# A two-layer hybrid encoder: attention of branch A beside later products, other places for transposing round trips, splits in halves

## The chip, the cores and the metric

The kernel runs on one core of one Trainium2 chip. The core has a matrix engine (TensorE, PE), a vector engine (VectorE, DVE), an activation engine (ScalarE, ACT), a general engine (GpSimd, POOL) and an engine that issues DMAs (SyncE, SP). Each works through its own instructions in a fixed order and waits on semaphores for the others. The metric is the device time of one execution in microseconds.

## The reference

Two layers of a mixer over 256 tokens of width 2048, in float32. In each layer the input is normalised, and one product with `w_in` (2048 x 16192) feeds three attention branches and their gates:

```python
h = _rmsnorm(x, g_pre)
u = h @ w_in
qa = (_rmsnorm(a_cq, a_g_cq) @ a_w_uq)      # A: latent attention, 8 heads
kva = (_rmsnorm(a_ckv, a_g_ckv) @ a_w_ukv)
o_a = _mla_attention(qn, qr, kn, kr, kva[..., A_NOPE:])
o_b = _rmsnorm(_diff_attention(bq, bk, bv, lam), b_g_sub) * (1.0 - lam_init)
o_c = _chunk_band_attention(cq, ck, cv, c_rel_bias)
branches = (o_a * silu(a_z), o_b * silu(b_z), o_c * silu(c_z))
y = sum(gates[:, :, n] * (branches[n] @ w_branch[n]) for n in range(3))
x = x + y @ w_out
```

In A the queries and keys come from two low-rank latents (cq, ckv) by second products (uq, ukv); queries and keys are normalised per head and part of them is rotated. B subtracts a second softmax map per head. C adds a relative bias.

## The kernel before

All products go through `matunit` (L150). It takes weights as a stream in the order that `stream_plan` (L43) writes down: blocks of 256 rows by 512 columns, one block per **step**. For a step SP issues one DMA of 512 KB into one of four buffers, ACT casts it to the matrix engine's fp32r type (high part, L166), DVE subtracts to get the low part (L167; three buffers each), and PE runs 12 matmuls: for each of two 128-row halves and two token tiles high x high, high x low, low x high (L176 to L178). A unit of 2048 rows is 8 steps; a pair of PSUM banks holds its two token tiles, and there are two pairs.

A layer's units come in this order: cq and ckv (A's latents), az0 and az1 (A's gate, two halves of four heads), then the second products uq0, ur, uk0, uv0 (half 0) and uq1, uk1, uv1 (half 1); B's k, q, v and z of half 0 and of half 1 (b0k ... b1z); four times a gate of A with its branch product br0; C's eight units; the gates and branch products of B and of C; four units of the output product.

Behind a unit of queries or keys stands `qk_natural` (L295): copies and squares on ACT, sums and scaling on DVE, the power on POOL. Then the result is needed with features on the partitions. There are two ways: `to_transposed` (L211) on PE, and `bounce` (L230), a round trip over DRAM: DVE transposes 32x32 blocks, one DMA writes 512 KB, four DMAs of 128 KB read it back in another order, and `from_bounced` (L277) casts and splits it into high and low part on ACT and DVE. `bounce` gets three numbers, the steps after its call at which the write, the read and the use are handed out: `later` (L140) notes them, and `run_due` (L144) runs what is due in `matunit`, between a step's cast and its matmuls (L169). The write and the read stand in SP's order behind that step's weight load, the use in ACT's order behind that step's cast (`tc.issue_after`).

Attention is `simple_half` (L428; A and C) and `diff_half` (L447; B): per head scores on PE, maximum on DVE, Exp on ACT, scaling, transposes of the map and products with v on PE, and a product with the gate. `silu_gate` (L342) makes that gate with Silu on ACT; `gate_branch` (L699) uses Sigmoid. `b_split` (L621) splits a finished branch for its branch product.

The code is traced from top to bottom, and a planner then fixes each engine's order before the run: earlier instructions have priority, and one that its model of times holds ready may go ahead of one that it holds not. What the order came to be can be read from the trace.

Of the kernel before, what the change touches and what calls it, by code (L numbers as in the profile page):

```python
# [8 lines left out]
F32 = mybir.dt.float32  # L9
# [9 lines left out]
NT = SEQ // P  # L19
# [23 lines left out]
def stream_plan():  # L43

    order = []
    for l in range(DEPTH):
        def win(name, lo, n):
            order.append(("w_in", l, lo, DM, n))
        win("cq", 0, 512)
        win("ckv", 512, 320)  # L50
        win("az", 832, 512)
        win("az", 832 + 512, 512)
        order.append(("uq", l, 0, 512, 512))
        order.append(("uq", l, 1024, 512, 512))
        order.append(("ukv", l, 0, 256, 512))
        order.append(("ukv", l, 1024, 256, 512))
        order.append(("uq", l, 512, 512, 512))
        order.append(("ukv", l, 512, 256, 512))
        order.append(("ukv", l, 1536, 256, 512))
        qb = 1856  # L60
        for hf in range(2):
            for s in (1, 0, 2, 3):
                win("b", qb + s * BW + hf * 512, 512)
        gb = 1856 + 8 * BW
        for j in range(4):
            win("g", gb + j * 512, 512)
            order.append(("br0", l, j * 512, BW, 512))
        qc = 1856 + 4 * BW
        for hf in range(2):
            for s in (1, 0, 3, 2):  # L70
                win("c", qc + s * BW + hf * 512, 512)
        for n in (1, 2):
            for j in range(4):
                win("g", gb + n * DM + j * 512, 512)
                order.append((f"br{n}", l, j * 512, BW, 512))
        for j in range(4):
            order.append(("out", l, j * 512, DM, 512))
    return order
# [3 lines left out]
def trunk_kernel(ctx: ExitStack, tc: tile.TileContext, x, xT, w, cols, rows, tab, bias, ident_d, out):  # L82
# [57 lines left out]
    def later(n, fn):  # L140

        due.append((state["n"] + n, fn))
# [87 lines left out]
    def bounce(src, name, at, then=None, dst=None):  # L230
# [23 lines left out]

        def use():
            with tc.issue_after(state["cast"].ins):
                then(flat)
            away.remove(name)

        later(at[0], write)  # L260
        later(at[1], read)
        if then is not None:
            later(at[2], use)
        return flat

    def bounced(z, b=None):

        v = z.rearrange("p (q b c) -> p q b c", b=HH, c=32)
        return v if b is None else v[:, :, b, :]

# [5 lines left out]

    def from_bounced(z, dh, dl, gain, per_block=False, put=None):  # L277

        if per_block:
            for b in range(HH):  # L280
                split(as_bounced(dh[:, b, :]), as_bounced(dl[:, b, :]), bounced(z, b), gain(b))
            return
        if gain is not None:
            nc.scalar.activation(z, z, AF.Copy, scale=gain)
        if put is not None:
            put(bounced(z), as_bounced)
        else:
            split(as_bounced(dh), as_bounced(dl), bounced(z))

# [46 lines left out]
    def vsplit(ps, rcol, name):  # L336
# [3 lines left out]
        return v  # L340

    def silu_gate(ps, rcol, name):  # L342
        z = zp.tile([P, NT, 512], F32, tag="z", name=name)
        for t in range(NT):
            nc.scalar.activation(z[:, t, :], ps[t], AF.Silu, scale=rcol[:, t:t + 1])
        return z
# [137 lines left out]
    for l in range(DEPTH):  # L484
# [85 lines left out]
        for t in range(NT):  # L570
# [6 lines left out]
        cqh, cql = abig[:, 0], abig[:, 1]  # L577
        bounce(ncq, f"cqT{l}", (9, 11, 14),
               lambda z: from_bounced(z, cqh, cql, lambda b: gcol(G_CQ + b), per_block=True))

# [40 lines left out]
        def b_split(z, hf, name, gain=None):  # L621
            bh[hf] = zp.tile([P, HH, SEQ], F32R, tag=f"bh{hf}", name=f"{name}h", bufs=1)
            bl[hf] = zp.tile([P, HH, SEQ], F32R, tag=f"bl{hf}", name=f"{name}l", bufs=1)
            assert not [x for x in away if x.startswith(name)]
            from_bounced(z, bh[hf], bl[hf], gain)

        za = [None, None]
        qr = [None, None]
        for hf in range(2):
            n = f"l{l}a{hf}"  # L630
            za[hf] = bounce(silu_gate(in_unit(f"az{hf}"), rcol, f"{n}z"), f"{n}zT", (7, 9))
        for hf in range(2):
            n = f"l{l}a{hf}"
            assert f"cqT{l}" not in away
# [19 lines left out]

            def parts(hl):
                qs = qr[hf][:, (hl % 2) * 2 + hl // 2, :]
                return [(qh[:, hl, :], kt2[:, :, hl, :], True), (qs, krt, True), (ql[:, hl, :], kt2[:, :, hl, :], False)]

            za[hf] = simple_half(za[hf], parts, v, lambda hl: mask_add, n)
        for hf in range(2):  # L660
            b_split(za[hf], hf, f"l{l}a{hf}")


        zb = [None, None]
        for hf in range(2):
            n = f"l{l}b{hf}"
            op = {}
            for i, nm in ((1, "k"), (0, "q")):
# [8 lines left out]
                else:  # L677
                    d = att_tile(f"{n}{nm}")
                    d = [d[:, 0], d[:, 1]]
                    put = lambda pt, v, d=d: split_stacked(v(d[0]), v(d[1]), pt)  # L680
                bounce(nat, f"{n}{nm}T", (11, 13, 15),
                       lambda z, i=i, put=put: from_bounced(z, None, None, cg[:, 1:2] if i == 0 else cg[:, 4:5], put=put))
                op[nm] = d
# [7 lines left out]
            diff_half(zb[hf], bparts, v, nlam, n)  # L691
            zb[hf] = bounce(zb[hf], f"{n}bT", (20, 22))

# [5 lines left out]
        def gate_branch(n):  # L699
            for j in range(4):  # L700
# [3 lines left out]
                g = wk.tile([P, NT, 512], F32, tag="g", name=f"{nm}g")  # L704
                for t in range(NT):
                    nc.scalar.activation(g[:, t, :], pg[t], AF.Sigmoid, scale=rcol[:, t:t + 1])
                pb = matunit(lambda kt: (bh[kt // 4][:, kt % 4, :], bl[kt // 4][:, kt % 4, :]), BW, 512, f"{nm}b")
# [6 lines left out]
                if n == 2:  # L714
                    yt = att_tile(f"{nm}y")
                    yh[j], yl[j] = yt[:, 0], yt[:, 1]
                    if j < 3:
                        yz = zp.tile([P, NT, 512], F32, tag="z", name=f"{nm}yz")
                        bounce(yacc[:, :, js], f"{nm}yT", (9, 11, 13),
                               lambda z, yt=yt: from_bounced(z, yt[:, 0], yt[:, 1], None), yz)  # L720
                    else:
                        to_transposed(lambda t: yacc[:, t, js], 4, yh[j], yl[j], None, f"{nm}yT")
# [7 lines left out]
        for hf in range(2):  # L730
# [8 lines left out]
            for i, nm in ((1, "k"), (0, "q")):  # L739
                nat = qk_natural(in_unit(f"c{hf}{nm}"), 128, rcol, f"{n}{nm}")  # L740
                th = op[nm] = att_tile(f"{n}{nm}")
                bounce(nat, f"{n}{nm}T", (8, 10, 12), lambda z, th=th, i=i: from_bounced(
                    z, th[:, 0], th[:, 1], cg[:, 2:3] if i == 0 else gcol(G_CKH)))
            zc[hf] = bounce(silu_gate(in_unit(f"c{hf}z"), rcol, f"{n}z"), f"{n}zT", (6, 8))
# [26 lines left out]
        for j in range(4):  # L771
# [11 lines left out]
            if more:  # L783
# [5 lines left out]
                if j < 3:  # L789
                    bounce(xres[:, :, js], f"x{l + 1}T{j}", (7, 9, 11),  # L790
                           lambda z, j=j, gx=gx: from_bounced(z, xg_next[0][j], xg_next[1][j], gx, per_block=True),
                           nat_pair(f"x{l + 1}n{j}"))
# [81 lines left out]
```

## Time and profile before

| | us |
|---|---|
| median of 3 runs (lowest to highest) | 2046.84 (2045.09 to 2046.86) |
| the profiled execution, its own time | 2047.27 |
| its span on the core | 2045.5 |
| PE busy | 1996.6 (98%) |
| DVE busy | 1262.2 (62%) |
| ACT busy | 1138.1 (56%) |
| POOL busy | 207.7 (10%) |

The span is what the trace covers; times of instructions are counted from its start. Busy is the share of the span in which an engine has an instruction in work; a matmul's end is modelled, so a busy PE may still run at its lower clock. The granted clock, 0.989 in the mean, is a share of full speed.

### The profile page before, as it was taken

What the parts mean: (1) busy time and instruction counts of PE and PEld (TensorE: products, weight loads), DVE (VectorE), ACT (ScalarE), POOL (GpSimd) and SP (SyncE); (2) the same over time, 40 slices, a digit from 0 to 9 for tenths busy, and PEclk for the clock granted to TensorE, in tenths of its full rate; (3) what the DMA queues carried; (4) which work ended last, traced back from release to release, by engine and by line L of the source; (5) the groups of instructions that cost most, each with busy time, mean ns of one, the idle gap of its engine ahead of it and who ended that gap; (6) DMA issues with size and microseconds to landing.
All of it is one profiled execution on the core that took longest, in us unless ns stands there. A gap on an engine that the chain in (4) does not pass through costs nothing.

```text
span 2045.5 us, 25426 instructions
## 1 busy us (share of the span) xinstructions
PE 1996.6 (98%) x9136; PEld 1656.8 (81%) x9136; DVE 1262.2 (62%) x1722; ACT 1138.1 (56%) x1634; POOL 207.7 (10%) x357
## 2 busy tenths in 40 slices
PE   9989998999999999999999899989999999999999
PEld 7868886788888888888888687777888888888887
DVE  5577776655665645566556787765556666555554
ACT  6566766544565544444456677566455665444443
POOL 2123040000100000000021130400010000000000
PEclk9989998999999999999999999999999999999999
DMA  8746566466768555678867365654668575556764
GB/s 291 242 130 177 186 198 195 159 207 214 244 179 254 174 192 195 213 229 263 265 214 227 123 185 175 215 166 163 215 199 256 182 241 175 196 193 208 239 244 155
DMA packets 160221, 418.24 MB, mean 204 GB/s; under 512 B 15056, under 2 KB 59088, under 8 KB 159328
## 3 DMA queue, kind: packets, MB, share of 16 engines
q1 hardware_dynamic: 157888, 407.66, 62.0%
q0 software_dynamic: 1920, 8.46, 1.3%
q8 instruction: 71, 1.16, 0.2%
q10 hardware_dynamic: 288, 0.52, 0.1%
q14 instruction: 54, 0.44, 0.1%
HBM read 391.93 MB, written 24.64 MB: 204 GB/s over the span
## 4 chain that ended last, share of the span: by engine, by line
PE 88%; DVE 4%; ACT 3%; DMA 2%; POOL 2%; issue 2%; SPq 0%; ACTq 0%; POOLq 0%; DVEq 0%
PE l0g_p L177 4%; PE l0g_p L178 4%; PE l0g_p L176 4%; PE l1g_p L177 4%; PE l1g_p L178 4%; PE l1g_p L176 4%; PE l0o_p L176 1%; PE l0o_p L177 1%; PE l0o_p L178 1%; PE l1o_p L177 1%; PE l1o_p L178 1%; PE l1o_p L176 1%; DMA l0cq_r<-w 1%; ACT L377 1%; PE l1az_p L177 1%
## 5 line engine op out<-in xcount | busy, mean ns | idle before, releaser
L167 DVE TENSOR_TENSOR l0g_l<-l0g_r,l0g_h 128x1024 fp32r<-128x1024 f32 x96 | 117.2, 1222 | 91.0 <-ACT l0g_h L166 90.9
L167 DVE TENSOR_TENSOR l1g_l<-l1g_r,l1g_h 128x1024 fp32r<-128x1024 f32 x96 | 117.2, 1222 | 90.9 <-ACT l1g_h L166 90.8
L166 ACT CAST l0g_h<-l0g_r 128x1024 fp32r<-128x1024 f32 x96 | 101.0, 1054 | 126.7 <-PE l0g_p L178 81.8
L166 ACT CAST l1g_h<-l1g_r 128x1024 fp32r<-128x1024 f32 x96 | 101.0, 1054 | 125.7 <-PE l1g_p L178 80.1
L177 PE MATMUL l0g_p<-l0g_l,xh 128*128 128x512 f32 x384 | 150.5, 392 | 0.5 <-DVE l0g_l L167 0.5
L178 PE MATMUL l0g_p<-l0g_h,xl 128*128 128x512 f32 x384 | 150.4, 392 | 0.0
L177 PE MATMUL l1g_p<-l1g_l,xh 128*128 128x512 f32 x384 | 149.8, 390 | 0.5 <-DVE l1g_l L167 0.5
L178 PE MATMUL l1g_p<-l1g_h,xl 128*128 128x512 f32 x384 | 149.7, 390 | 0.0
L176 PE MATMUL l0g_p<-l0g_h,xh 128*128 128x512 f32 x384 | 136.2, 391 | 0.0
L176 PE MATMUL l1g_p<-l1g_h,xh 128*128 128x512 f32 x384 | 135.8, 390 | 0.0
L177 PEld LDWEIGHTS l0g_p<-l0g_l,xh 128*128 128x128 f32 x384 | 72.6, 189 | 15.6 <-DVE l0g_l L167 0.7
L178 PEld LDWEIGHTS l0g_p<-l0g_h,xl 128*128 128x128 f32 x384 | 72.5, 189 | 15.0
L177 PEld LDWEIGHTS l1g_p<-l1g_l,xh 128*128 128x128 f32 x384 | 72.1, 188 | 15.4 <-DVE l1g_l L167 0.7
L178 PEld LDWEIGHTS l1g_p<-l1g_h,xl 128*128 128x128 f32 x384 | 72.1, 188 | 14.9
L176 PEld LDWEIGHTS l0g_p<-l0g_h,xh 128*128 128x128 f32 x384 | 72.1, 188 | 14.7
L176 PEld LDWEIGHTS l1g_p<-l1g_h,xh 128*128 128x128 f32 x384 | 71.9, 188 | 14.6
L167 DVE TENSOR_TENSOR l1o_l<-l1o_r,l1o_h 128x1024 fp32r<-128x1024 f32 x32 | 39.2, 1225 | 40.5 <-ACT l1o_h L166 40.4
L166 ACT CAST l1o_h<-l1o_r 128x1024 fp32r<-128x1024 f32 x32 | 33.8, 1055 | 52.2 <-PE l1o_p L178 47.2
L167 DVE TENSOR_TENSOR l0o_l<-l0o_r,l0o_h 128x1024 fp32r<-128x1024 f32 x32 | 39.1, 1221 | 33.5 <-ACT l0o_h L166 33.3
L166 ACT CAST l0o_h<-l0o_r 128x1024 fp32r<-128x1024 f32 x32 | 33.7, 1053 | 44.1 <-PE l0o_p L178 36.5
L377 ACT ACT_TABLE_LOAD x18 | 23.1, 1283 | 19.2 <-DVE l0a_mx L375 5.7
L764 POOL DMA_DIRECT2D xres<-xscr x1 | 0.8, 792 | 311.1 <-PE l1n2j3yT_t L217 311.1
(1626 smaller groups left out, 5867.8 us busy)
## 6 DMA issues: line engine op xcount, KB each, us to landing
l0g_r<-w SPq DMA_DIRECT2D x96, 512.0 KB, 3.5
l1g_r<-w SPq DMA_DIRECT2D x96, 512.0 KB, 3.4
l0o_r<-w SPq DMA_DIRECT2D x32, 512.0 KB, 4.5
l1o_r<-w SPq DMA_DIRECT2D x32, 512.0 KB, 3.9
l0az_r<-w SPq DMA_DIRECT2D x16, 512.0 KB, 4.5
l1az_r<-w SPq DMA_DIRECT2D x16, 512.0 KB, 4.4
l0b0k_r<-w SPq DMA_DIRECT2D x8, 512.0 KB, 3.3
l0b0q_r<-w SPq DMA_DIRECT2D x8, 512.0 KB, 3.2
```

Source lines behind the costliest of these rows:

```text
L166: state["cast"] = nc.scalar.copy(wh[:, ks, :N], wr[:, ks, :N])
L167: nc.vector.tensor_tensor(out=wl[:, ks, :N], in0=wr[:, ks, :N], in1=wh[:, ks, :N].bitcast(F32), op=ALU.subtract)
L176: nc.tensor.matmul(ps[t][:, :N], h[:, ts], wh[:, k2, :N], start=first, stop=False)
L177: nc.tensor.matmul(ps[t][:, :N], h[:, ts], wl[:, k2, :N], start=False, stop=False)
L178: nc.tensor.matmul(ps[t][:, :N], lo[:, ts], wh[:, k2, :N], start=False, stop=last)
L377: nc.scalar.activation(p[:, o], so, AF.Exp, bias=mx[:, t:t + 1], scale=-1.0, accum_out=sums[:, t:t + 1])
L764: nc.gpsimd.dma_start(xres, x_src.rearrange("(t p) d -> p t d", p=P))
```

## The change

The weight stream is reordered with the units: half 0's second products stand between az0 and az1, half 1's behind az1. Attention of A is handed to `later`, ten steps after the end of az0 and of az1, and `b_split` goes with it. `bounce` hands its use out in two halves (blocks 0 and 1, then 2 and 3 a step later); `from_bounced` works on such a half, and with a scalar gain folds the scale into the cast. Several round trips get other steps. Silu and Sigmoid are taken for token tile 1 first, with tile 0 bound behind it.

```diff
-        win("az", 832 + 512, 512)
         order.append(("uq", l, 0, 512, 512))
         order.append(("uq", l, 1024, 512, 512))
         order.append(("ukv", l, 0, 256, 512))
         order.append(("ukv", l, 1024, 256, 512))
+        win("az", 832 + 512, 512)
...
-        def use():
+        def use(b0):
             with tc.issue_after(state["cast"].ins):
-                then(flat)
-            away.remove(name)
+                then(flat, slice(b0, b0 + 2))
+            if b0:
+                away.remove(name)
...
-            later(at[2], use)
+            later(at[2], lambda: use(0))
+            later(at[2] + 1, lambda: use(2))
...
+    def from_bounced(z, bs, dh, dl, gain, put=None):
+        if put is not None:
+            nc.scalar.activation(bounced(z, bs), bounced(z, bs), AF.Copy, scale=gain)
+            put(bounced(z, bs), lambda d: as_bounced(d[:, bs, :]))
+        elif gain is None:
+            split(as_bounced(dh[:, bs, :]), as_bounced(dl[:, bs, :]), bounced(z, bs))
+        else:
+            one = not callable(gain)
+            if one:
+                nc.scalar.activation(as_bounced(dh[:, bs, :]), bounced(z, bs), AF.Copy, scale=gain)
+            for b in range(bs.start, bs.stop):
+                g = gain if one else gain(b)
+                h, lo, zb = as_bounced(dh[:, b, :]), as_bounced(dl[:, b, :]), bounced(z, b)
+                if not one:
+                    nc.scalar.activation(h, zb, AF.Copy, scale=g)
+                nc.vector.scalar_tensor_tensor(out=lo, in0=zb, scalar=g, in1=h.bitcast(F32),
+                                               op0=ALU.mult, op1=ALU.subtract)
...
+    def gates(z, ps, rcol, func):
+        i = nc.scalar.activation(z[:, 1, :], ps[1], func, scale=rcol[:, 1:2])
+        with tc.issue_after(i.ins):
+            nc.scalar.activation(z[:, 0, :], ps[0], func, scale=rcol[:, 0:1])
...
-        bounce(ncq, f"cqT{l}", (9, 11, 14),
+        bounce(ncq, f"cqT{l}", (9, 11, 14) if l else (4, 6, 7),
...
         for hf in range(2):
             n = f"l{l}a{hf}"
-            za[hf] = bounce(silu_gate(in_unit(f"az{hf}"), rcol, f"{n}z"), f"{n}zT", (7, 9))
-        for hf in range(2):
-            n = f"l{l}a{hf}"
+            za[hf] = bounce(silu_gate(in_unit(f"az{hf}"), rcol, f"{n}z"), f"{n}zT", (6, 8))
+            az_end = state["n"]
...
-            za[hf] = simple_half(za[hf], parts, v, lambda hl: mask_add, n)
-        for hf in range(2):
-            b_split(za[hf], hf, f"l{l}a{hf}")
+            def attention(hf=hf, parts=parts, v=v, n=n):
+                b_split(simple_half(za[hf], parts, v, lambda hl: mask_add, n), hf, n)
+            later(az_end + 10 - state["n"], attention)
...
-                bounce(nat, f"{n}{nm}T", (11, 13, 15),
+                at = (11, 13, 15) if hf == 0 else (16, 18, 20) if nm == "k" else (12, 14, 15)
+                bounce(nat, f"{n}{nm}T", at, lambda z, bs, i=i, put=put: from_bounced(
...
-            zb[hf] = bounce(zb[hf], f"{n}bT", (20, 22))
+            zb[hf] = bounce(zb[hf], f"{n}bT", (28, 30))
```

## Rows read from the trace of the kernel before

**Rows 1.** The page: busy time of PE, DVE, ACT and POOL.
```profile
PE 1996.6 (98%) x9136; PEld 1656.8 (81%) x9136; DVE 1262.2 (62%) x1722; ACT 1138.1 (56%) x1634; POOL 207.7 (10%) x357
```
**Rows 2.** Waits of PE: line waited for; us in total, times, longest.
```profile
PE l1b1z_p L176 <- ACT l1b1z_h L166: 4.5, 1, 4.5
PE l1a_s L358 <- DVE l1a0k L188: 3.7, 1, 3.7
PE l0b1z_p L176 <- ACT l0b1z_h L166: 3.5, 1, 3.5
PE l0a_s L358 <- DVE l0a0k L188: 3.4, 1, 3.4
PE l1b_s L358 <- ACT l1b_e L377: 3.1, 2, 2.0
PE l0b_s L358 <- ACT l0b_e L377: 3.0, 2, 2.0
...
PE l0a1uv_p L176 <- ACT l0a1k_n L301: 2.7, 1, 2.7
PE l0n0j0b_p L176 <- ACT l0n0j0b_h L166: 2.1, 1, 2.1
...
PE l0a0kT_t L217 <- DVE abig L197: 1.8, 1, 1.8
PE l1a0kT_t L217 <- DVE abig L197: 1.7, 1, 1.7
```
**Rows 3.** Windows: stretch, length, PE busy (count), granted clock, DMA share, GB/s.
```profile
130.90:138.90 8.00, 8.00 (x31) 0.62 0.00 0
315.80:323.80 8.00, 7.24 (x21) 0.66 0.69 172
351.00:359.00 8.00, 7.49 (x28) 0.79 0.58 197
382.00:390.00 8.00, 7.47 (x28) 0.79 0.59 196
...
1396.60:1404.60 8.00, 7.84 (x21) 0.58 0.61 191
```
**Rows 4.** Timeline of PE, layer 0: start, duration, engine, line, operation.
```profile
91.34 0.39 PE L176 MATMUL l0a0uq_p<-l0a0uq_h,abig 128*128 128x512 f32 x1
...
96.78 0.39 PE L176 MATMUL l0a0ur_p<-l0a0ur_h,abig 128*128 128x512 f32 x1
```
**Rows 5.** Windows for DVE: az1 and A's second products.
```profile
69.00:91.00 22.00, 12.88 (x15) 1.00 0.80 259
91.00:131.00 40.00, 34.25 (x48) 0.95 0.60 186
```
**Rows 6.** Groups of DVE from 91 to 133 us: busy, mean ns, idle before.
```profile
L197 DVE TENSOR_TENSOR abig<-l0a0rT_t,abig 64x512 fp32r<-64x512 f32 x4 | 2.7, 686 | 0.1
...
L332 DVE TENSOR_TENSOR l0a0rr_b<-l0a0r_n,rt 128x256 f32<-128x256 f32 x2 | 0.8, 414 | 0.0
```
**Rows 7.** Lines 345 and 706 on ACT: ns min/median/max, first and last start.
```profile
L345 ACT ACT_TABLE_LOAD  x14: 1283/1283/1283, 68.2 to 1662.4; - x14
...
L345 ACT ACTIVATE l0b1z<-l0b1z_p,rcol x2: 687/689/691, 343.1 to 347.0; 128x512 f32<-128x512 f32 x2
...
L706 ACT ACTIVATE l0n0j0g<-l0g_p,rcol x2: 687/688/688, 374.3 to 378.1; 128x512 f32<-128x512 f32 x2
```
**Rows 8.** Timelines of ACT and SP, round trip of b1's k in layer 0.
```profile
309.29 1.15 ACT L284 ACTIVATE l0b1k_n<-l0b1k_n,cgain 128x1024 f32<-128x1024 f32 x1 [4.06 <-DMA l0b1k_n<-l0b1kT_scr]
...
299.46 0.38 SPq L245 DMA_DIRECT2D l0b1kT_scr<-l0b1kT_tu  x1
```
**Rows 9.** Round trip of cq, layer 0: DVE, SP, and DMA issues (us to landing).
```profile
46.12 0.71 DVE L238 STREAM_TRANSPOSE cqT_tu<-ncq 128x512 f32<-128x512 f32 x1 [0.18 <-ACT ncq L575]
...
61.75 1.81 SPq L251 DMA_DIRECT2D ncq<-cqT_scr  x4
...
cqT_scr<-cqT_tu SPq DMA_DIRECT2D x2, 512.0 KB, 5.7
```

## The prediction before the result was known

> **What bounds the kernel now.** I read the page's busy times first: TensorE (PE) is busy for 1996.6 of 2045.5 us, VectorE (DVE) for 62% and ScalarE (ACT) for 56% [rows 1]. The number of matmuls does not change, so two things can be won: the 48.9 us in which PE stands, and whatever it loses while its clock is low. Second, the waits of PE [rows 2]: twelve rows hold 34.3 of the 48.9 us (ten are shown; product uv1 and br0 of layer 1 repeat those of layer 0 to the tenth), and they lie at four places, once per layer each: the end of branch A's products (scores, kT transposes, product uv1), 3.7 + 3.4 + 2.7 + 2.7 + 1.8 + 1.7 = 16.0 us; b1z's products, which wait for a cast on ACT, 4.5 + 3.5 = 8.0 us; branch B's scores, which wait for an exponential on ACT, 3.1 + 3.0 = 6.1 us; and the first product br0 after the first gate, 2.1 + 2.1 = 4.2 us.
>
> Third, the granted clock in the 8 us behind each such place [rows 3]. It is 0.58 to 0.79 of full there, which is a mix of the 2.4 GHz level and the 1.2 GHz one after PE stood. 8 us times what is missing from 1 gives 3.0, 2.7, 1.7 and 1.7 us in layer 0, and the same windows of layer 1 give 2.9, 2.9, 0 and 3.4 (eight windows, the first four and the last are shown). That is 5.9 us for A, 5.6 for b1z, 1.7 for B's scores, 5.1 for the gate: 18.3 in all. So the four places cost 21.9, 13.6, 7.8 and 9.3 us, together 52.6; this is the most that these edits can win there, and the rest of PE's idle time (start, small waits) is out of their reach.
>
> **The change part by part.** One step of the stream (256 rows of a 512-column weight block) is 12 matmuls: product uq0, two steps, lasts from 91.34 to 96.78, so a step is 2.72 us [rows 4].
>
> **A's order and its attention.** Before, az0 and az1 run first, and from 69 to 91 us, under az1, DVE is busy for 12.9 of 22 us only; then all seven latent products come in a row and DVE is busy for 34.3 of 40 us [rows 5], with PE standing for its results. After, the four products of half 0 (6 steps) stand ahead of az1 (8 steps, 21.8 us), and az1's own successors are 4 steps and then b0k. So each half's norms, rotations and transposes get other products to lie beside. What DVE needs for it: half 0's chain is 19.6 us in 14 groups of 30 instructions [rows 6]; half 1's first instructions and the low-part subtractions of the weights, about 1 us a step, are the rest of the 34.3. From az0's end to az1's end there are now 14 steps, 38 us; 20 + 14 = 34 us of DVE work fit, but at 89%. By that the scores of half 0 become ready near az1's end, though they are handed out after the fourth step of az1. If the planner's order puts az1's products ahead of them nothing waits; if it puts them at that fourth step, PE meets them 27 us after az0's end with 30 to 34 us of DVE work ahead (10 or 14 steps' subtractions): 3 to 7 us of wait. Bounds for what remains of A's 21.9 us: 0 and all; I take 4 us per layer, 8, so **14 are won**.
>
> **The Silu of az1** now comes while attention of half 0 uses Exp, so ACT loads tables twice more per layer: 2 x 1.283 us [rows 7]. Beside 8 steps of products it costs nothing unless a cast behind it is late; cover gone, it is 2.6 us per layer. I take 0.
>
> The Trainium skill (ScalarE: Activation LUTs, "Table sets: the hidden batching unit") says to finish all calls of one set before going to another, and this edit does the contrary; its section "What ACT_TABLE_LOAD costs" prices a switch at about 2.66 us, the load and a drain. By that the added pair is an estimated 5.3 us per layer; felt in full, it would take 10.6 of the 14 us, and the time would be about 2018, which lies within rival 1's bounds. The trace agrees on the load (1283 ns in all 14) but leaves no room for the drain: the 3.9 us between the two Silus of b1z hold a Silu of 0.69 and two loads of 2.57 us, which leaves 0.64 us for the exponential between them [rows 7].
>
> **gates().** A Silu or Sigmoid of token tile 0 is ready three matmuls, 0.7 us, before that of tile 1, and the planner put exponentials between: the two Silus of b1z start 3.9 us apart, the two Sigmoids of the first gate 3.8 us, where one takes 0.69 [rows 7]. With tile 1 first and tile 0 bound behind it, both are ready together and two of four loads go: 2.57 us per place, at b0z, b1z and the first gate. The waits there are 2.0 us at most for one score and 2.1 for br0 [rows 2], so all of them fit into 2.57; what is late next is the next cast, on time elsewhere. Bounds: 0 (the planner still separates them) and 17.1; of 7.8 and 9.3 I take **7 and 8 won**.
>
> **b1's k round trip, 11/13/15 to 16/18/20 steps, the second half a step later.** Before, ACT stood 4.06 us on the landing of k's read at 309.29, and the casts of b1z behind it in ACT's order were late; the write had left SP only at 299.46 [rows 8], since k's norm runs behind b0's attention. Five steps are 13.6 us, over three times the wait, and the write leaves no later than its data allow. The use falls into b1z's steps 4 and 5; ACT has its casts there, and half of k's scale and casts in each. **B1's q, 12/14/15** moves write and read by one step, its use stays. **The round trip of B's outputs, 20/22 to 28/30**, moves one write and four reads of b0 past b1v's and b1z's first loads on SP into b1z's steps 4 and 6, where b1q's stand too: SP issues two times four reads (1.81 us for four [rows 9]) in a row, and b1z's loads 7 and 8 are behind them. For b1 they move past two more gate steps, far ahead of use. Bounds: all 13.6 won, or 3 us per layer late again at load 7; I take 2 us lost of 13.6, **11.6 won**.
>
> **cqT in layer 0, 9/11/14 to 4/6/7 and 8.** One write, four reads, four casts and four subtractions move up by some 20 us, ahead of uq0, which must have them. The source is transposed at 46.12 + 0.71 = 46.8; the write lands 5.7 us later, 52.5; the four reads take SP 1.81 us and, at the same landing time, are there at 60.0 [rows 9]. az0 ends 8 steps before uq0 of the kernel before: 91.3 - 21.8 = 69.6, so the use has 9.6 us for 8 short instructions. Behind the read SP holds az0's seventh and eighth load: they land at 60.1, are cast and subtracted 2.3 us later, and PE wants the seventh at 69.6 - 5.4 = 64.2. That is hidden by 1.8 us; without cover it is 1 to 3 us, once. I take 0. The write of az0's result (6 and 8 in place of 7 and 9) is similar: two Silus, a load, two transposes 4 us after az0's end, landing at 9.7, the read issued by 11.5, az1's third load ready at 19.5 and wanted at 8 x 2.72 = 21.8. Hidden by 2.3 us; 1 us per layer if not.
>
> **Splits in halves.** A 128x1024 scale is 1.15 us [rows 8], a 128x512 activation 0.69 [rows 7], so a halved one costs 1.38: 0.2 us more each. With a scalar gain the scale is folded into the cast, one pass over the data less. Both lie on an ACT that is idle for 44% and are bounded by -1 and +2 us over the kernel; I take 0, and for small new waits of all kinds 1 us.
>
> Sum: 14 + 7 + 8 + 11.6 - 1 = 39.6 us. The profiled execution took 2047.27 us, 1.8 beyond its span; 2047.3 - 39.6 = 2007.7, and the median of the runs is 0.4 lower than the profiled one, so **2007 us**. Its own range is 1993 (everything at the four places goes) to 2018.
>
> **The rivals.**
>
> **Rival 1.** A's wait stays, elsewhere. DVE is the limit of A, and the same 20 us of chain per half now meet attention of half 0 as well. For it: 34.3 of 40 us busy. Against: DVE's idle 9 us under az1, which the new order uses. Then A wins 0 to 5 in place of 14, and az1's Silu costs its 2.6 per layer: 2007 + 9 to 19 = 2016 to 2026, say 2023.
>
> **Rival 2.** The edits don't meet the order. The planner parts Silus as before and A waits as before; only b1z's 11.6 stand against 3 us per layer at load 7, 3 at cqT and the Silu's 2.6 per layer, 14.2 together: 2043 to 2051, about 2049. Against it: three of the four places have separate causes.
>
> **Rival 3.** Slower: PE waits at every head. PE takes its instructions in a fixed order. Attention inside az1, uq1 and b0k is four heads of exp, transposes and sums per half, and where the planner has their steps closer together than a DVE at 89% can serve, each head costs one wait like that on an exponential, 2.0 us [rows 2], twice (scores, then values): 4 heads x 2 halves x 2 layers x 4 us = 64 us, against 26.6 won elsewhere: about 2085 at full price; it decides from 26.6 + 4 us on, that is from half of that price. Against it: attention of A beside b0k before shows no such wait among PE's.
>
> **How the numbers follow.** My forecast 0.52, rival 1 0.26, rival 2 0.07, rival 3 0.11, and 0.04 for still better than 1993. What the measurement can tell from no change is about 0.2%, 4 us. Faster by more than that: 0.52 + 0.26 + 0.04 = 0.82; rival 2 gives the 0.06 of the same and 0.01 of slower; slower 0.12. The range to hold 8 in 10 runs from 1992 to 2034, over the forecast and rival 1 with its bounds.
>
> **What would show it.** Right: no wait for a b1z cast or for an exponential among PE's longest; Silus and Sigmoids in pairs under 0.8 us apart; idle PE near 20 us in all; a clock of 1.00 behind the four places. A's step is wrong if waits of PE for DVE at A's scores, values or transposes still sum to over 8 us; the SP step if PE waits for casts of az1's third or b1z's seventh block that waited for DMA; the cqT step if uq0 starts after a wait. A time above 2034 or an idle PE above 45 us would make the prediction wrong.

## The result, and the profile after

The changed kernel takes 1992.99 us in the median (1991.75 to 1995.01), the kernel before 2046.17 in the same series: a ratio of 0.9742, 95% interval 0.9725 to 0.9758, or 53.2 us less. That is 14 us below the forecast of 2007, and about the 52.6 us that the prediction had named as the most to be won at the four places. The span of the profiled execution is 1991.0 us, with a mean granted clock of 0.999.

The page's busy times, after (answers to [rows 1]):

```profile
PE 1976.5 (99%) x9136; PEld 1646.7 (83%) x9136; DVE 1266.5 (64%) x1796; ACT 1118.1 (56%) x1668; POOL 214.6 (11%) x357
```

PE stands for 1991.0 - 1976.5 = 14.5 us where it stood 48.9, which is 34.4 us less. And the same 9136 matmuls are busy for 20.1 us less: the clock, whose mean rose from 0.989 to 0.999, by 1%. Together they are the 54.5 us by which the span fell. The waits of PE, after (us in total, times, longest; answers to [rows 2]):

```profile
PE l0b1z_p L176 <- ACT l0b1z_h L166: 1.6, 1, 1.6
...
PE l1b_s L370 <- ACT l1b_e L389: 1.1, 1, 1.1
...
PE l0b_s L370 <- ACT l0b_e L389: 0.7, 1, 0.7
PE l0b1z_p L177 <- DVE l0b1z_l L167: 0.5, 1, 0.5
PE l0a_s L370 <- DVE l0a0k L188: 0.4, 1, 0.4
```

Of A's 16.0 us, 0.8 are left (the last row, and its like in layer 1); product uv1, the kT transposes and br0 are gone from the list; of the 8.0 at b1z's casts, 1.6, in layer 0 alone; of the 6.1 at B's scores, 1.8. The windows of PE behind the four places of layer 0, after (columns as in [rows 3]):

```profile
111.00:119.00 8.00, 7.97 (x43) 1.00 0.56 192
317.90:325.90 8.00, 7.99 (x31) 0.79 0.52 180
328.00:336.00 8.00, 7.34 (x35) 1.00 0.29 90
356.00:364.00 8.00, 8.00 (x41) 1.00 0.37 126
```

Only behind the one wait that is left, at b1z, is the clock still low, 0.79.

**A.** Timeline of PE where A's half 0 begins its scores, and windows of DVE ahead of that:

```profile
111.03 0.39 PE L370 MATMUL l0a_s<-l0a0k,l0a0q 128*128 128x256 f32 x1 [0.43 <-DVE l0a0k L188]
```
```profile
86.00:90.00 4.00, 4.00 (x7) 1.00 0.47 161
...
94.00:98.00 4.00, 4.00 (x6) 1.00 0.72 243
```

DVE is full for 12 us under az1, as it was before from 111 to 131 us (busy for 19.8 of 20 us), but PE has az1's matmuls to do meanwhile. The scores stand at az1's end, where their operands are ready but for 0.43 us, though the code hands them out four steps earlier.

**The tables of ACT.** Groups of table loads, after, and ACT's timeline at az1's gate and at b1z's (answer to [rows 7]):

```profile
L351 ACT ACT_TABLE_LOAD x16 | 20.5, 1283 | 1.2 <-PE l1g_p L178 0.5 <-PE l0g_p L178 0.5
L389 ACT ACT_TABLE_LOAD x12 | 15.4, 1283 | 3.1 <-DVE l1a_mx L387 0.9 <-DVE l0a_mx L387 0.9 <-DVE l0c_mx L387 0.6
```
```profile
111.61 0.71 ACT L351 ACTIVATE l0a1z<-l0az_p,rcol 128x512 f32<-128x512 f32 x1
...
114.76 1.28 ACT L389 ACT_TABLE_LOAD   x1 [0.92 <-DVE l0a_mx L387]
...
326.98 1.28 ACT L351 ACT_TABLE_LOAD   x1
328.28 0.69 ACT L351 ACTIVATE l0b1z<-l0b1z_p,rcol 128x512 f32<-128x512 f32 x1
328.86 0.68 ACT L353 ACTIVATE l0b1z<-l0b1z_p,rcol 128x512 f32<-128x512 f32 x1
```

The two Silus of b1z start 0.58 us apart in place of 3.9. There are 28 loads where the trace of before has 40 on its three lines of Silu, Sigmoid and Exp. The Silus of az1 need none: they come, at 111.61 and 112.18, before half 0's first exponential, which fetches its table only at 114.76.

**b1z, layer 0.** ACT, SP and PE at the wait that is left (answer to [rows 8]):

```profile
315.55 1.04 ACT L166 CAST l0b1z_h<-l0b1z_r 128x1024 fp32r<-128x1024 f32 x1 [2.85 <-DMA l0b1z_r<-w]
```
```profile
297.16 0.43 SPq L245 DMA_DIRECT2D l0b0bT_scr<-l0b0bT_tu  x1
...
303.98 1.81 SPq L251 DMA_DIRECT2D l0b0z<-l0b0bT_scr  x4
305.88 3.55 SPq L251 DMA_DIRECT2D l0b1q_n<-l0b1qT_scr  x4
309.95 1.06 SPq L165 DMA_DIRECT2D l0b1z_r<-w  x2
```
```profile
316.65 0.73 PE L176 MATMUL l0b1z_p<-l0b1z_h,xh 128*128 128x512 f32 x2 [1.57 <-ACT l0b1z_h L166]
```

B's output and b1's q go out together (297.16 and 297.69) and come back together; b1z's loads 7 and 8 stand behind both in SP's order, and the cast of load 7 waits for its landing. SP also stands still ahead of the reads, until the write that they read from has landed:

```profile
SPq L251 <- DMA l0b0bT_scr<-l0b0bT_tu: 3.0, 1, 3.0
```

So the two loads have this wait ahead of them, and 5.4 us from the first read to the last.

### The profile page after: what moved, and what is told of

The parts are those of the page before. It is cut to its first block, busy times and chain, and to the rows that moved or that the text cites. A ratio compares the mean times of both kernels' runs of the same rounds, so it can differ in the third digit from the quotient of the medians.

```text
span 1991.0 us, 25510 instructions
## 1 busy us (share of the span) xinstructions
PE 1976.5 (99%) x9136; PEld 1646.7 (83%) x9136; DVE 1266.5 (64%) x1796; ACT 1118.1 (56%) x1668; POOL 214.6 (11%) x357
## 4 chain that ended last, share of the span: by engine, by line
PE 93%; DMA 3%; ACT 1%; POOL 1%; DVE 1%; issue 1%; SPq 0%; ACTq 0%; POOLq 0%; DVEq 0%
PE l1g_p L177 4%; PE l1g_p L178 4%; PE l0g_p L177 4%; PE l1g_p L176 4%; PE l0g_p L178 4%; PE l0g_p L176 4%; PE l0o_p L178 1%; PE l0o_p L177 1%; PE l0o_p L176 1%; PE l1o_p L177 1%; PE l1o_p L178 1%; PE l1o_p L176 1%; DMA l0cq_r<-w 1%; PE l1az_p L178 1%; PE l0az_p L178 1%
## 5 line engine op out<-in xcount | busy, mean ns | idle before, releaser
L177 PEld LDWEIGHTS l0g_p<-l0g_l,xh 128*128 128x128 f32 x384 | 72.2, 188 | 14.5
L177 PEld LDWEIGHTS l1g_p<-l1g_l,xh 128*128 128x128 f32 x384 | 72.1, 188 | 14.5
```

The lines of the kernel that those rows point to most:

```text
L177: nc.tensor.matmul(ps[t][:, :N], h[:, ts], wl[:, k2, :N], start=False, stop=False)
```

## The experiments

Times of different series are compared by their ratio to the kernel before, run in the same series; 0.001 of it is 2.05 us.

### Each part alone

The four parts of the change, each put by itself into the kernel before; all four together are the changed kernel.

**A's order and postponed attention** (with the places of cqT and of az's results):

```diff
+        win("az", 832 + 512, 512)
...
+            later(az_end + 10 - state["n"], attention)
```

> The kernel before with A's part alone (order of products, attention handed out ten steps after az0 and az1, cq's and az's round trips in their new places). Theory 1, four places that add up: A's place held 21.9 us, of which nearly all goes, so 2025 to 2028 us (20 +/- 2 won), with the waits at b1z, at B's scores and at the first br0 left as they were. Rival, A's earlier end also relieves B's chain: the b1z wait shrinks too and more than 28 us are won, below 2018. Rival, A's gain needs the other parts (halves): under 14 won, above 2032.

2023.95 us, ratio 0.9895 (0.988 to 0.9909): 21.8 us won. A's waits are gone, and those at br0 stay. At b1z and at B's scores the waits shift without going: b1z's casts 3.5 us in place of 8.0, its low parts 3.8 in place of 1.4, the scores 8.0 in place of 6.1. All that A cost was won, not two thirds.

**gates():**

```diff
-            for t in range(NT):
-                nc.scalar.activation(g[:, t, :], pg[t], AF.Sigmoid, scale=rcol[:, t:t + 1])
+            gates(g, pg, rcol, AF.Sigmoid)
```

> The kernel before with the paired Silus and Sigmoids alone. Theory 1: the waits of PE at B's scores (6.1 us) and at the first br0 (4.2) go with their clock loss (6.8): 14 to 17 us won, 2029 to 2033, and 12 table loads fewer. Rival, the loads were hidden and the waits come from somewhere else in that stage: under 5 won.

2028.88 us, ratio 0.9921 (0.9906 to 0.9936): 16.9 won, at the top of what was expected. The waits at B's scores are off the list; at br0 1.0 and 0.7 us are left of 2.1 each. But the loads of the three lines fell from 40 to 32 and not by the 12 expected. ACT at the first gate of layer 0, before and in this kernel:

```profile
380.53 1.03 ACT L166 CAST l0n0j0b_h<-l0n0j0b_r 128x1024 fp32r<-128x1024 f32 x1
```
```profile
367.78 0.69 ACT L344 ACTIVATE l0n0j0g<-l0g_p,rcol 128x512 f32<-128x512 f32 x1
...
371.63 0.69 ACT L346 ACTIVATE l0n0j0g<-l0g_p,rcol 128x512 f32<-128x512 f32 x1
372.22 1.04 ACT L166 CAST l0n0j0b_h<-l0n0j0b_r 128x1024 fp32r<-128x1024 f32 x1
```

Binding fixes which of the two comes first, not that nothing stands between them. Here the two Sigmoids still start 3.85 us apart, with two loads between. What did change is that the cast behind them comes 0.6 us after the start of the second, where before it came 2.5 us after (378.06 [rows 7], then 380.53). Only in the changed kernel are the Sigmoids of the first gate a pair (354.72 and 355.30).

**The places of B's round trips:**

```diff
+                at = (11, 13, 15) if hf == 0 else (16, 18, 20) if nm == "k" else (12, 14, 15)
...
-            zb[hf] = bounce(zb[hf], f"{n}bT", (20, 22))
+            zb[hf] = bounce(zb[hf], f"{n}bT", (28, 30))
```

> The kernel before with branch B's round trips in their new places alone, uses in one piece. Theory 1: the b1z wait of 8.0 us and 5.6 of clock go, less a new wait on late weight loads of about 2: 10 to 13 us won, 2033 to 2037. Rival, the use in one piece (5.4 us of ACT in a row) stops the casts at its new place as well: under 6 won.

2038.38 us, ratio 0.9962 (0.9948 to 0.9977): 7.4 won, short of the 10 to 13. ACT's timeline and PE's waits in this kernel:

```profile
324.50 1.15 ACT L284 ACTIVATE l0b0z<-l0b0z,cgain 128x1024 f32<-128x1024 f32 x1 [2.29 <-DMA l0b0z<-l0b0bT_scr]
325.56 1.98 ACT L166 CAST l0b1z_h<-l0b1z_r 128x1024 fp32r<-128x1024 f32 x2
```
```profile
PE l0b1z_p L176 <- ACT l0b1z_h L166: 3.8, 1, 3.8
...
PE l1b1z_p L176 <- ACT l1b1z_h L166: 2.8, 1, 2.8
```

k's wait is gone, and another has its place: the first thing that `b_split` does with B's output is to scale it in place (L284). That needs nothing but the data, and the planner puts it among b1z's casts, and there ACT now stands on its landing, with two casts of b1z behind it. In the kernel before the same scaling ran at 300.25 and waited 0.19 us, since its trip had been early.

**Halves and the folded gain:**

```diff
-        if gain is not None:
-            nc.scalar.activation(z, z, AF.Copy, scale=gain)
...
+                nc.scalar.activation(as_bounced(dh[:, bs, :]), bounced(z, bs), AF.Copy, scale=gain)
```

> The kernel before with the splits in two halves alone, all places old. Theory 1: within 2 us of the kernel before, since the b1z wait there comes from the landing of a read and not from the length of the use. Rival, the halves are what frees the casts: 4 us or more won, all at b1z.

2038.69 us, ratio 0.9966 (0.9955 to 0.9978): 7.1 won where next to nothing was expected. PE's waits in this kernel:

```profile
PE l1b1z_p L176 <- ACT l1b1z_h L166: 4.0, 1, 4.0
...
PE l0b1z_p L176 <- ACT l0b1z_h L166: 2.9, 1, 2.9
...
PE l1b_s L365 <- ACT l1b_e L384: 1.6, 2, 1.0
PE l1b_o L406 <- ACT l1b_pp L184: 1.5, 1, 1.5
PE l0b_o L406 <- ACT l0b_pp L184: 1.5, 1, 1.5
...
PE l0b_s L365 <- ACT l0b_e L384: 1.2, 2, 0.7
```

The waits for b1z's casts fall little, from 8.0 to 6.9 us. Those at B's scores fall from 6.1 to 2.8 us, but B's products with v now wait for ACT's cast of the map, 3.0 us in both layers, where they did not before. In all PE stands for 4.2 us less, spread over several waits, and is busy for 5.6 us less at the same work. Which of the two edits does this, and how, no run here shows.

The four gains alone are 21.8, 16.9, 7.4 and 7.1: 53.2 in sum, as much as the whole change gives. Each of them is known to 2 to 3 us, so the parts add up within several us; that it comes out to the tenth is chance.

### One part taken back out of the changed kernel

**Without the new places of B's round trips** (k and q of half 1 11, 13, 15 and output 20, 22 again):

> The changed kernel with branch B's round trips at their old places (k 11, 13, 15 for both halves, output 20, 22); halves and the folded gain stay. Theory of the landing (b1's k is read too early for its write, ScalarE stands on it, and b1z's casts behind it are late): the waits at b1z come back, 2.9 + 1.4 and 4.0 + 0.5 us as with the halves alone, and their clock with them, 7 to 13 us slower than the changed kernel: 2000 to 2006 us. Rival (the halves and the fold had already taken most of it, and the places only shift the wait to load 7): within 4 us of 1993.

1998.56 us, ratio 0.9765 (0.9745 to 0.9785): 4.7 us slower than the changed kernel by the ratios' middles, with intervals that overlap. The waits did come back: PE's, in this kernel:

```profile
PE l1b1z_p L176 <- ACT l1b1z_h L166: 5.1, 1, 5.1
PE l0b1z_p L176 <- ACT l0b1z_h L166: 3.9, 1, 3.9
```

The mechanism is that of the prediction; the price is less than expected. With these waits in place those at B's scores (1.8 us in the changed kernel) and at layer 1's first gate product are off the list, so that idle PE grows by 4.3 us only, from 14.5 to 18.8.

**Without halves and folding** (the diff of that part, backwards):

> The changed kernel with the old single-piece use of what comes back from DRAM, and with the gain scaled in place before the split (three of the change's four parts). Theory F (what the fourth part is worth is that the gain of branch B's output is folded into the cast that writes bh, so that ScalarE can't take it up inside product b1z): 4 to 7 us slower than the changed kernel, 1997 to 2000 us; in ScalarE's queue the scaling of l0b0z stands between the casts of b1z and waits 2 to 3 us for its DMA, and TensorE's wait at b1z in layer 0 is 3 us or more in place of 1.6 + 0.5. Theory H (it is the halving): the same time, but the wait stands at k's single-piece casts and not at the scaling of l0b0z. Theory O (the parts overlap, and the places alone take the wait away): within 2 us of 1993.

1999.74 us (1995.51 to 2001.82), ratio 0.9779 (0.9765 to 0.9792): 7.6 us slower than the changed kernel. The place was as theory F said, the wait not: in the profiled execution, the fastest of the five at 1995.51 us, the scaling stands between two casts of b1z but waits only 0.62 us. So this trace does not show the loss that the median has.

**Halves without folding, folding without halves:**

```diff
             if one:
-                nc.scalar.activation(as_bounced(dh[:, bs, :]), bounced(z, bs), AF.Copy, scale=gain)
+                nc.scalar.activation(bounced(z, bs), bounced(z, bs), AF.Copy, scale=gain)
+                split(as_bounced(dh[:, bs, :]), as_bounced(dl[:, bs, :]), bounced(z, bs))
+                return
```
```diff
-            later(at[2], lambda: use(0))
-            later(at[2] + 1, lambda: use(2))
+            later(at[2], use)
...
-            for b0 in (0, 2):
-                from_bounced(z, slice(b0, b0 + 2), bh[hf], bl[hf], gain)
+            from_bounced(z, slice(0, HH), bh[hf], bl[hf], gain)
```

The first edit takes the folding back for every scalar gain, so for C's queries and keys as well. In the second, `use` hands out all four blocks at once.

> The changed kernel, halves kept, but the gain is scaled in place on each half and the split follows (no folding). Theory F: as without halves, 1997 to 2000 us; ScalarE waits 2 to 3 us for the DMA of l0b0z between two casts of b1z, then finishes those casts late. Theory H: 1992 to 1995 us, no wait of TensorE at b1z over what the changed kernel has (1.6 + 0.5).

> The changed kernel, gain folded into the cast, but all that comes back is used in one piece. Theory F: 1992 to 1995 us; TensorE's wait at b1z in layer 0 no more than 0.7 us longer than in the changed kernel, since only k's single-piece scale and casts (some 3 us of ScalarE) stand among the casts of b1z. Theory H: 1997 to 2000 us, with a wait of 3 us at b1z behind k's casts, which stand together in one piece.

1995.87 us, ratio 0.976 (0.9747 to 0.9773), and 1995.48, ratio 0.9756 (0.9743 to 0.9769): 3.7 and 2.9 us slower than the changed kernel by the middles, with intervals that overlap. By time neither theory wins: each edit seems to be worth about half of the 7.6 us. By the traces they differ. ACT and PE's waits in the one without folding:

```profile
311.59 0.72 ACT L288 ACTIVATE l0b0z<-l0b0z,cgain 128x512 f32<-128x512 f32 x1 [4.64 <-DMA l0b0z<-l0b0bT_scr]
```
```profile
PE l0b1z_p L176 <- ACT l0b1z_h L166: 3.2, 1, 3.2
PE l1b1z_p L176 <- ACT l1b1z_h L166: 2.5, 1, 2.5
```

The scaling waits 4.64 us in layer 0 and 4.04 in layer 1, and PE behind it in both; with folding and without halves no wait of PE for a cast of b1z on ACT is listed, and 1.5 and 1.2 us for its low parts from DVE. The first trace is of the slowest of four executions (1998.22 us), the second of the fastest (1994.75), so the place of the wait is shown, and its size for a usual execution is not.

### The place of B's output trip

**Six steps later:**

```diff
-            zb[hf] = bounce(zb[hf], f"{n}bT", (28, 30))
+            zb[hf] = bounce(zb[hf], f"{n}bT", (34, 36))
```

> The changed kernel with the round trip of B's output 6 steps later again (write 34, read 36 steps on). Theory of the queue (in layer 0 the write of B's output stands in SP's queue ahead of q's write and of the loads 7 and 8 of b1z, and the cast of load 7 waits for it): TensorE's waits at b1z in layer 0 (1.6 + 0.5 us) fall under 0.5 in sum and the time is 2 to 3 us lower, 1990 to 1991 us; no wait appears where B's half 0 is used, since that lies at the first gate's product. Rival (the loads are late by themselves, since the window for b1z's weights opens too late): the waits stay and the time is 1993. Rival 2 (the later write collides with the attention of B's half 1 or with the gate's loads): slower than 1993, with a wait of TensorE at the first g product.

1985.46 us (1985.2 to 1986.17), ratio 0.9708 (0.9694 to 0.9721): faster than the changed kernel, by 7.0 us, and the best version here. Its busy times, SP in the same stretch, and the first of PE's waits:

```profile
PE 1973.5 (99%) x9136; PEld 1644.8 (83%) x9136; DVE 1266.3 (64%) x1796; ACT 1118.4 (56%) x1668; POOL 215.3 (11%) x357
```
```profile
303.59 0.87 SPq L165 DMA_DIRECT2D l0b1z_r<-w  x2
...
309.31 0.43 SPq L245 DMA_DIRECT2D l0b0bT_scr<-l0b0bT_tu  x1
```
```profile
PE wps L133 <- DVE warm L130: 1.4, 1, 1.4
PE l0ckv_p L176 <- ACT l0ckv_h L166: 1.1, 1, 1.1
```

Loads 7 and 8 of b1z leave SP at 303.59 in place of 309.95, and b1z has no wait. The theory was right on that, but its 2 to 3 us were too few: idle PE fell by 4.6 us (14.5 to 9.9; 2.1 of it at b1z, the rest in waits of about 1 us or less, such as the 0.8 us at layer 1's first gate product), and busy PE by 3.0, of which the window with 0.79 accounts for 1.7.

**The same, without halves and folding** (the single-piece use and in-place scaling of the kernel before):

> The kernel with the latest trip of B's output (34, 36), but with the single-piece use and the scaling in place of the kernel before. Theory F (the in-place scaling of B's output is taken up early in ScalarE's queue and stands there on its DMA): the wait goes along with the trip, since the scaling now stands behind the second cast of product g; ScalarE waits for the DMA of l0b0z there, the casts of g and the exponentials of B's scores behind it are late, TensorE waits 2 us or more at g or at the scores, and the time is 1990 to 1997. Theory C (what the fourth part saved was only the meeting of that trip with b1z's loads and casts): no wait over 1 us at b1z, g or the scores, 1985 to 1988 us, as with the halves.

2002.37 us, ratio 0.9784 (0.9771 to 0.9798): 15.6 us slower than with them, and beyond what theory F expected. ACT's timeline and PE's waits:

```profile
326.52 1.15 ACT L284 ACTIVATE l0b0z<-l0b0z,cgain 128x1024 f32<-128x1024 f32 x1 [5.24 <-DMA l0b0z<-l0b0bT_scr]
327.58 0.34 ACT L382 ACTIVATE l0b_e<-l0b_s,l0b_mx 128x128 f32<-128x128 f32 x1
```
```profile
PE l0b_s L363 <- ACT l0b_e L382: 4.7, 1, 4.7
PE l1b_s L363 <- ACT l1b_e L382: 3.8, 1, 3.8
```

The wait went along with the trip. The scaling now stands 5.24 us between two exponentials of B's scores, and 4.40 us in layer 1. As the halves are out here too, the 15.6 us are the price of both edits, not of the scaling alone. Where the folded form of the same work runs shows ACT's timeline in the changed kernel:

```profile
457.85 1.34 ACT L288 ACTIVATE l0b0h<-l0b0z,cgain 128x512 fp32r<-128x512 f32 x2 [1.44 <-PE l0n0j3b_p L177]
```

It writes into bh, which A's branch products read until product l0n0j3b; its turn comes at 457.85, released by that product, 154 us after the read was issued. The kernel before shows both forms on the same data: the scaling in place ran at 300.25, and the cast into bh, which stands right behind it in the code, only at 483.1. That is why folding protects: not by the pass over the data that it saves, but by the place in ACT's order that the new destination forces.

### A: the order or the postponement

**The products in their old order, attention postponed** (half 0 by 8 steps, half 1 by 10; the places of cqT and az's results as before). The edit of the postponement:

```diff
-            later(az_end + 10 - state["n"], attention)
+            later(8 if hf == 0 else 10, attention)
```

**The new order, half 0's attention in its place** (so that az0's result is back by then, its round trip moves up by two steps):

```diff
-            za[hf] = bounce(silu_gate(in_unit(f"az{hf}"), rcol, f"{n}z"), f"{n}zT", (6, 8))
+            za[hf] = bounce(silu_gate(in_unit(f"az{hf}"), rcol, f"{n}z"), f"{n}zT", (6, 8) if hf else (4, 6))
...
-            later(az_end + 10 - state["n"], attention)
+            if hf == 0:
+                attention()
+            else:
+                later(az_end + 10 - state["n"], attention)
```

> The changed kernel with A's products in the order of the kernel before (az0, az1, then the seven latent products; the places of cqT and of az's results as before), but with each half's attention put off, half 0 by 8 steps and half 1 by 10. Theory P (postponement is what took A's waits away: TensorE no longer meets scores whose operands VectorE has not finished; the order of the products only gives VectorE more cover, which it needs little of): 1993 to 1997 us, waits of TensorE at A's scores, kT transposes and uv1 together under 3 us. Theory O (the order is needed: in the old order all of A's chains come in 14 steps, where VectorE was busy 34.3 of 40 us before): 4 to 10 us slower than the changed kernel, 1997 to 2003, with waits of TensorE for VectorE or ScalarE at uv1, at half 1's kT transposes (2 to 5 us per layer) and the clock below 1 behind them.

> The changed kernel with its new order of A's products, but attention of half 0 directly behind uv0 (half 1 as changed). Theory P: the scores of half 0 are met while VectorE still works on half 0's chain (in the changed kernel it is at 4.00 of 4 us from 86 to 98 us, and those scores started at 111), so TensorE waits at A's scores in both layers, 3 to 8 us per layer and 1 to 3 of clock behind it: 2001 to 2015 us. Theory O: 1993 to 1997 us, since the planner lays az1's products ahead of scores that are not ready.

The old order: 2014.78 us, ratio 0.9846 (0.9828 to 0.9863), 21 us slower than the changed kernel, which is all of A's gain and twice the most that theory O expected. PE's waits in it:

```profile
PE l0a1qT_t L217 <- DVE l0a0k L188: 3.9, 1, 3.9
...
PE l0a1uv_p L176 <- ACT l0a1k_n L308: 2.7, 1, 2.7
```

Postponing moved the wait from the scores (3.4 us before) to the transposes of half 1's queries (3.9); the wait of uv1 did not change by a tenth. The new order with half 0's attention in place: 1994.35 us, ratio 0.9741 (0.9723 to 0.976), the same as the changed kernel. PE at half 0's scores:

```profile
110.54 0.39 PE L370 MATMUL l0a_s<-l0a0k,l0a0q 128*128 128x256 f32 x1 [0.43 <-DVE l0a0k L188]
```

Handed out directly behind uv0, which ended near 86 us, the scores still stand behind all of az1. Theory P, that the postponement does it, fell in both runs: the order of the products does, and for half 0 the planner does the postponing. Half 1 was not tried in place. The old places of cqT and az's results came back together with the old order, but none of the waits above is one for their data.

## Why the prediction was right or wrong

| term | forecast, us | alone | taken out again |
|---|---|---|---|
| A | 14 | 21.8 | 21 (old order) |
| gates(): scores and gate | 7 + 8 | 16.9 | not run |
| B's places | 11.6 | 7.4 | 4.7 |
| halves and folding | 0 | 7.1 | 7.6 |
| small waits | -1 | | |
| sum | 39.6 | 53.2 | |

The misses are +7.8, +1.9, -4.2, +7.1 and +1, which is the 13.6 us between 39.6 and 53.2. The time lies only 1 us inside the range, near its lower end of 1992; the forecast's own range ends at 1993, where everything at the four places goes, and that is about what came.

**What bounds the kernel** held: 34.4 us of idle PE and 20.1 of clock went, where the four places had been read as 34.3 and 18.3. That the first two agree to the tenth is luck: 4.2 us of waits are left at the four places (0.8, 1.6, 1.8 and 0), so 30.1 were won there, and 4.3 at small waits which the prediction had put out of reach.

**A: the wrong value between two ends.** The prediction said that the scores would be ready near az1's end (they were, at 111.03), that nothing waits if the planner puts az1 ahead, and 3 to 7 us per layer if not. The step that failed is "I take 4 us per layer, 8". It was the lower end, 0.4 us; what the upper one would have cost, no run shows. DVE's share was also higher than the 89% of the prediction, since a low-part subtraction takes 1.22 us and not about 1: 19.6 us and 14 times 1.22 are 36.7 of the 38 us, and the scores were 0.43 us short of ready. There was no need to choose: the planner lets what its model holds ready go ahead of what it holds not, and the run with attention in place shows that it did so across 8 steps of products.

**The Silu of az1** was priced at 0, rightly, for a wrong reason. The two added table loads per layer do not exist, since both Silus run before the first exponential; with A's part alone there are 40 loads, as before. The Trainium skill's advice against changing sets (ScalarE: Activation LUTs, "Table sets: the hidden batching unit") was not violated here, so the 5.3 us per layer that the prediction had estimated from its price had nothing to stand on. The drain that the Trainium skill names beside the load (ScalarE: Activation LUTs, "What ACT_TABLE_LOAD costs") does not show in the trace of after either: a load of 1.28 us begins at 326.98, 0.01 us after the instruction before it ends, and the Silu starts 0.02 us after the load's end, at 328.28.

**gates()** was nearly right in size, 16.9 for 15. The cause holds at b1z: in the run of this part alone its two Silus start 0.58 us apart, and the scores behind do not wait. At the first gate it is not shown: in that run the Sigmoids stayed apart and no load was saved there, yet the wait fell from 2.1 to 1.0 us in layer 0 and the clock in the 8 us behind it rose from 0.79 to 1.00. By the trace the earlier cast is the likely cause, and no run parts it from the rest.

**k's trip and the output's trip** were right in both parts of their mechanism: k's wait went, and load 7 was late, 1.57 + 0.53 us behind two times four reads on SP. By the prediction's own sign (PE waits for the cast of b1z's seventh block, which waited for its DMA) the step on SP is wrong; but the loss had been allowed for, with 2 us. Forecast for both layers, it came in layer 0 only, and with the clock of 0.79 behind it it is 3.8 us. The wait of 3.0 us for the write's landing is not in the prediction's account of SP, which has the reads alone. What the prediction did not see is the scaling in place, which takes back part of the gain if it is left in: with the places alone b1z keeps 6.6 us of waits for casts, and 7.4 are won in place of 11.6. With the trip at 34 and 36 b1z has no wait at all.

**Halves and folding: the step that failed outright.** "Both lie on an ACT that is idle for 44% and are bounded by -1 and +2 us" priced the instructions by their durations. An instruction that waits for a DMA costs the queue behind it its wait, not its 1.15 us: 2.29, 4.64 and 5.24 us in the traces of three kernels, though only 0.62 in a fourth, which is slower in the median all the same. Where it met the exponentials, the kernel without the part is 15.6 us slower. That explains why folding is needed together with the later trip. What the halving is worth beside it has a time, 2.9 us inside overlapping intervals, and no cause. Nor is the 7.1 us explained that the part wins alone, where the scaling had waited 0.19 us only; there the waits at B's scores move to B's products with v, and which of the two edits wins the time stays open.

**Hidden moves** were hidden: no wait at uq0 for cqT, none in az1 for az's round trip.

**The rivals** did not come: A's waits did not stay (rival 1), the edits met the order (rival 2), and the attention of half 0 came behind az1 and not inside it, where no head of it made PE wait for over 0.5 us (rival 3).

## What to carry to other kernels

An operation in place on data that comes from a DMA has no other condition than the landing, so a planner may take it up early and put the whole wait into an engine's order; let its first use write to the buffer where it is wanted, and it is held back until that is free. When a wait is to go, look for cover by putting independent products between producer and consumer (here 21 us); handing the consumer out later does not help where the products behind it wait for the same engine. Two instructions bound in order can still have others between them, so read from the trace whether a pair came to be one. And when a trip is moved, read what stands behind its reads in the DMA-issuing queue: here six more steps were worth another 7 us.

## What the runs showed that was not expected

Two kernels in which ACT stands on landings vary by 6.3 us over five and six runs: 1995.5 to 2001.8 us with the scaling in place at 28 and 30, and 2035.1 to 2041.4 with the places alone. The fastest kernel, where PE waits at none of b1z's casts, varies by 1.0 over four (1985.2 to 1986.2). That the landings make the difference is not shown: the kernel without folding, with the wait of 4.64 us, varies by 2.9 over four. But one profile of such a kernel can miss the loss that its median has.
